# Strassen's seven products for 26 up blocks, planes reloaded in their own place, the first norm by splits

## The chip, the cores and the metric

The kernel runs on one core of a Trainium2 chip. The time is device microseconds from the start to the end of one execution; that of a kernel is the median of several runs. The engines are named as in the profile: PE (matrix unit), PEld (its weight loads), DVE (vector engine), ACT (scalar engine), POOL (a second vector engine), SP (it issues most DMAs). Each engine works through its own queue in order.

## The reference

One inference step of one hybrid decoder layer over 1024 prompt tokens and 8 sample tokens of width 1024: two branches (HGRN2 and Mamba-2) on a normed input, a gated merge, an output projection, and then a feed-forward part (FFN) of inner width 4096, which is where most of the change lies. Everything is float32.

```python
h = _rmsnorm(x, p['norm_mix']) * (1 + sc1) + sh1
proj = h @ p['w_in']
q, f, i, og, z, xbc, dt, ga, gb = jnp.split(proj, IN_OFFSETS, axis=-1)
...
u = jax.nn.sigmoid(ga + bma) * (o_hg @ p['w_br_a']) + jax.nn.sigmoid(gb + bmb) * (y @ p['w_br_b'])
x = x + g1 * (u @ p['w_out'])
h2 = _rmsnorm(x, p['norm_mlp']) * (1 + sc2) + sh2
x = x + g2 * (jnp.square(jax.nn.relu(h2 @ p['w_up'])) @ p['w_down'])
```

## The kernel before

Activations lie transposed: a plane is 128 channels (partitions) by NT = 1032 tokens (1024 prompt and 8 sample), so a width of 1024 is 8 planes. Tokens are cut in NS = 3 splits of SW = 344 columns. A weight block is 128 output channels: a tile of 128 x 1024 that holds 8 blocks of 128 x 128.

Precision is kept by splitting each float32 operand into a high part `hi` (rounded to float32r, on ACT) and a low part `lo` (the rest, on DVE). Each product is then three float32r matmuls, wh·xl, wl·xh and wh·xh. One output block thus takes 3 splits x 8 k-blocks x 3 = 72 matmuls of 344 columns.

`load_w` brings a weight tile into a staging buffer (`stage`, name `wr`, three buffers), and makes `wh` (line 53, ACT) and `wl` (line 55, DVE), two buffers each, at a high priority. `dense_split` (line 86) computes one split, `dense` three. `DenseK` (line 114) instead takes one plane of the input after the other into three or six open accumulators; it is used where the planes only just become ready: at the first norm, and at the two merge products.

The stages in order: modulation (ada) and first norm with the first DenseK (`phase_h`), HGRN2, SSM groups, the merge (`phase_merge`: last gates, `w_br_a`, `w_br_b`), `w_out`, the FFN, a last norm. In the merge, o- and y-planes (`od`, `yd`) and gate planes (`gd`) come back from DRAM; `load_split` loads a plane into a staging buffer and splits it. In the FFN, four chunks follow each other: 8 up blocks, whose results (relu, square) are split and kept in SBUF as `ah`, `al`, then 8 down blocks that read them and add to `x1`.

The program is written with tiles: a scheduler orders each engine's instructions by their priority, and a tile's next writer waits for the readers of the buffer that it reuses. Planes lie in pools by tag ("A", "Q1", "Q2", "Q3").

Of the kernel before, what the change touches and what calls it, by code (L numbers as in the profile page):

```python
# [17 lines left out]
P = 128  # L18
T = 1024
# [18 lines left out]
def cs(s):  # L38
    return slice(s * SW, (s + 1) * SW)


def stage(k):
    return k.wp.tile([P, NT], F32, tag="wr", name="wr", bufs=3)


def load_w(k, src, prio=AHEAD):

    nc = k.nc
    with k.tc.high_priority(prio):
# [3 lines left out]
        nc.scalar.activation(wh, wr, AF.Copy)  # L53
        wl = k.wp.tile([P, KD * P], F32R, tag="wl", name="wl", bufs=2)
        nc.vector.tensor_tensor(wl, wr, wh.bitcast(F32), op=ALU.subtract)  # L55
    return wh, wl
# [21 lines left out]
def dense_split(k, w, X, s, evac, M=P):  # L78
    wh, wl = w
    nc = k.nc  # L80
    acc = k.ps.tile([P, 512], F32, tag="acc", name="acc", bufs=3)
    n = len(X)
    for i, (xh, xl) in enumerate(X):
        sl = slice(i * M, (i + 1) * M)
        for j, (a, b) in enumerate(((wh, xl), (wl, xh), (wh, xh))):
            nc.tensor.matmul(acc[:M, :SW], a[:, sl], b[:, cs(s)],  # L86
                             start=(i == 0 and j == 0), stop=(i == n - 1 and j == 2))
    with k.tc.high_priority(AHEAD):
        evac(s, acc[:M, :SW])


def dense(k, src, X, evac):

    w = load_w(k, src)
    for s in range(NS):
        dense_split(k, w, X, s, evac)


class DenseK:
# [8 lines left out]
    def step(self, xh, xl):  # L108
        k, i = self.k, self.i
        sl = slice(i * P, (i + 1) * P)  # L110
        for (wh, wl), ac in zip(self.ws, self.accs):
            for s in range(NS):
                for j, (a, b) in enumerate(((wh, xl), (wl, xh), (wh, xh))):
                    k.nc.tensor.matmul(ac[s][:, :SW], a[:, sl], b[:, cs(s)],  # L114
                                       start=(i == 0 and j == 0), stop=(i == self.n - 1 and j == 2))
        self.i += 1
        if self.i < self.n:
            return
        with k.tc.high_priority(AHEAD):
            for ev, ac in zip(self.evacs, self.accs):  # L120
                for s in range(NS):
                    ev(s, ac[s][:, :SW])


def split_plane(k, src, tag, hi_name="hi", lo_name="lo"):
    nc = k.nc
    hi = k.pp.tile([P, NT], F32R, tag=tag, name=hi_name)
    nc.scalar.activation(hi, src, AF.Copy)
    lo = k.pp.tile([P, NT], F32R, tag=tag, name=lo_name)
    nc.vector.tensor_tensor(lo, src, hi.bitcast(F32), op=ALU.subtract)  # L130
    return hi, lo
# [146 lines left out]
def phase_h(k, evacs):  # L278


    nc = k.nc
    X = []

    def plane(tag, name):
        return k.pp.tile([P, NT], F32, tag=tag, name=name)
    ss = [rec_ps(k, "ss") for s in range(NS)]
    SUMS = ((0, 1, 2, 3), (4, 5, 6), (7,))
    for kk in range(KD):
        x = plane("B", "x")
# [24 lines left out]
    ws = [ada_load(k, n, (wa(), wa())) for n in range(AH)]  # L314
    for s in range(NS):
        sl = cs(s)
        rstd_from(k, ss[s][:, :SW], SW, 1.0 / 1024, (ra[:, sl], rs[:, sl], rt[:, sl]))
    k.hX = []

    def plane_step(kk):  # L320
        A, sh = scale_shift(k, k.i, kk, k.norm_mix, 0, 8)
        x = X[kk]
        hi = k.pp.tile([P, NT], F32R, tag="A", name="hh")
        lo = k.pp.tile([P, NT], F32R, tag="A", name="hl")

        nc.gpsimd.tensor_tensor(x[:, T:], x[:, T:], A[:, 1:9], op=ALU.mult)
        nc.gpsimd.tensor_tensor(x[:, T:], x[:, T:], rs[:, T:], op=ALU.mult)
        nc.gpsimd.tensor_tensor(x[:, T:], x[:, T:], sh[:, 1:9], op=ALU.add)
        nc.vector.scalar_tensor_tensor(x[:, :T], x[:, :T], A[:, 0:1], rs[:, :T], ALU.mult, ALU.mult)
        nc.scalar.activation(hi[:, :T], x[:, :T], AF.Identity, bias=sh[:, 0:1])  # L330
        nc.scalar.activation(hi[:, T:], x[:, T:], AF.Copy)
        nc.vector.scalar_tensor_tensor(lo[:, :T], x[:, :T], sh[:, 0:1], hi[:, :T].bitcast(F32),
                                       ALU.add, ALU.subtract)
        nc.gpsimd.tensor_tensor(lo[:, T:], x[:, T:], hi[:, T:].bitcast(F32), op=ALU.subtract)
# [495 lines left out]

def load_split(k, src, tag, r=None):
# [29 lines left out]
def phase_merge(k):  # L863
# [8 lines left out]
    oX = []  # L872
    for i in range(KD):
        with k.tc.high_priority(AHEAD):
            oX.append(load_split(k, k.od[i], "A", stage(k)))
        d.step(*oX[i])
    for m in range(2, KD):
        u.append(load_gate(k, m, "Q1"))
# [109 lines left out]
    return x1, h2  # L988


def phase_ffn(k, x1, h2):
    nc = k.nc
    for c in range(4):
        aX, evacs = [], []
        for j in range(KD):
            tag = "A" if j < 4 else "Q3"
            hi = k.pp.tile([P, NT], F32R, tag=tag, name="ah")
            lo = k.pp.tile([P, NT], F32R, tag=tag, name="al")

            def evac(s, ps, hi=hi, lo=lo):  # L1000
                r = k.sp2.tile([P, SW], F32, tag="mt", name="r", bufs=2)
                nc.scalar.activation(r, ps, AF.Relu)  # L1002
                nc.vector.tensor_tensor(r, r, r, op=ALU.mult)  # L1003
                nc.scalar.activation(hi[:, cs(s)], r, AF.Copy)
                nc.vector.tensor_tensor(lo[:, cs(s)], r, hi[:, cs(s)].bitcast(F32), op=ALU.subtract)  # L1005
            evacs.append(evac)
            aX.append((hi, lo))
        up = k.i["w_up"][c * KD:(c + 1) * KD]
        if c == 0:

            ws = [load_w(k, up[j]) for j in range(2)]
            for j, s in [(j, s) for j in range(2) for s in LAST[:2]] + [(0, LAST[2]), (1, LAST[2])]:
                dense_split(k, ws[j], h2, s, evacs[j])
        for j in range(0 if c else 2, KD):
            dense(k, up[j], h2, evacs[j])

        def add(m):
            return lambda s, ps: gated_add(k, s, x1[m][:, cs(s)], x1[m][:, cs(s)], ps, k.modT[:, 40 + m, :])
        if c < 3:
            for m in range(KD):  # L1020
                dense(k, k.i["w_down"][c * KD + m], aX, add(m))
            continue
        for s in LAST:
            acc = k.sp2.tile([P, SW], F32, tag="sqa", name="sqa", bufs=1)
            for m in range(KD):
                w = load_w(k, k.i["w_down"][c * KD + m])
                dense_split(k, w, aX, s, add(m))
                sum_sq(k, acc, x1[m][:, cs(s)], m == 0)
            y = rstd_model(k, acc)
            for m in range(KD):  # L1030
                xx = x1[m][:, cs(s)]
                nc.vector.scalar_tensor_tensor(xx, xx, k.norm_final[:, m:m + 1], y, ALU.mult, ALU.mult)
                nc.sync.dma_start(k.o["y"][m][:, cs(s)], xx)

# [172 lines left out]
```

## Time and profile before

| | us |
|---|---|
| median of three runs | 2561.46 (2558.68 to 2564.11) |
| the profiled execution, its own time | 2561.21 |
| its span | 2559.4 |
| PE busy | 2503.3 (98%) |
| DVE busy | 1642.1 (64%) |
| ACT busy | 1042.8 (41%) |
| first L114 matmul on PE | 35.23 |
| first merge DenseK (`w_br_a` 0 and 1) | 1450.87 to 1473.5 |
| second merge DenseK (`w_br_b` 8 and 9) | 1633.52 to 1656.2 |
| FFN matmuls | about 1820 to 2545 |

Times within an execution are microseconds from the start of its span. The page's chain names what the end waited for, step by step; a row of groups gives line, engine, operation, names, shape, count, busy time and mean ns, and behind the last bar the idle time before it. PE's durations are modelled; its starts are measured, so the interval between two starts is what a matmul costs in a row.

### The profile page before, as it was taken

The numbers are of one execution on the slowest core, as the hardware profiler recorded it, in microseconds if no ns is written. First come the engines' busy times: TensorE is split into PE (matmuls) and PEld (weight loads), VectorE is DVE, ScalarE is ACT, GpSimd is POOL, SyncE is SP. The second block draws the span as 40 slices with busy tenths as digits, with TensorE's granted clock in tenths as the row PEclk, the third lists the DMA queues.
The fourth block names the chain that finished last, engine by engine and source line by source line (L and its number), as shares of the span: only waits on it lengthen the run. The fifth ranks groups of instructions, "written<-read, shape, count | busy, mean of one in ns | idle before, by whom it ended". The sixth has DMA issues, their size and how long they took to land.

```text
span 2559.4 us, 46195 instructions
## 1 busy us (share of the span) xinstructions
PE 2503.3 (98%) x19470; PEld 2439.2 (95%) x19470; DVE 1642.1 (64%) x3314; ACT 1042.8 (41%) x1566; POOL 18.1 (1%) x48
## 2 busy tenths in 40 slices
PE   6999999999999999999999999999999999999998
PEld 5999999889999999999999999999999999999997
DVE  6788888887587687787787744457732332332356
ACT  4455555555444544545545532224520220221333
POOL 2000000000000000000000000000000000000000
PEclk9999999999999999999999999999999999999999
DMA  6322222323333243243343554234211111111134
GB/s 252 102 100 101 101 100 101 101 95 93 93 125 120 90 150 119 99 143 125 101 143 120 195 166 147 75 108 144 88 50 50 42 50 50 42 50 48 43 102 146
DMA packets 92496, 267.04 MB, mean 104 GB/s; under 512 B 16592, under 2 KB 23568, under 8 KB 92272
## 3 DMA queue, kind: packets, MB, share of 16 engines
q1 hardware_dynamic: 91744, 263.08, 31.4%
q8 instruction: 153, 2.51, 0.4%
q0 software_dynamic: 112, 0.66, 0.1%
q14 instruction: 55, 0.45, 0.1%
q10 hardware_dynamic: 432, 0.35, 0.0%
HBM read 224.12 MB, written 40.19 MB: 103 GB/s over the span
## 4 chain that ended last, share of the span: by engine, by line
PE 77%; DVE 2%; ACT 1%; issue 0%; DVEq 0%; ACTq 0%
PE acc L86 68%; PE acc L114 2%; PE y_ps L791 1%; PE yi_ps L795 1%; PE kvx_ps L755 1%; PE xt_ps L743 1%; PE cb_ps L725 1%; DVE wl L55 0%; PE btok_ps L718 0%; PE ss L160 0%; ACT wh L53 0%; PE acc L610 0%; PE ss L161 0%; PE ss L948 0%; DVE sqa L942 0%
## 5 line engine op out<-in xcount | busy, mean ns | idle before, releaser
L86 PE MATMUL acc<-hl,wh 128*128 128x344 f32 x2232 | 720.1, 323 | 0.0
L86 PE MATMUL acc<-hh,wh 128*128 128x344 f32 x2232 | 719.9, 323 | 0.0
L86 PE MATMUL acc<-hh,wl 128*128 128x344 f32 x2232 | 719.3, 322 | 0.0
L86 PEld LDWEIGHTS acc<-hh,wh 128*128 128x128 f32 x2232 | 420.0, 188 | 3.6 <-issue 1.6
L86 PEld LDWEIGHTS acc<-hl,wh 128*128 128x128 f32 x2232 | 419.4, 188 | 3.2
L86 PEld LDWEIGHTS acc<-hh,wl 128*128 128x128 f32 x2232 | 419.3, 188 | 2.8 <-issue 1.4
L53 ACT ACTIVATE wh<-wr 128x1024 fp32r<-128x1024 f32 x224 | 236.5, 1056 | 437.1 <-PE acc L86 360.0
L55 DVE TENSOR_TENSOR wl<-wr,wh 128x1024 fp32r<-128x1024 f32 x224 | 274.1, 1224 | 216.8 <-ACT wh L53 215.9
L86 PE MATMUL acc<-ah,wl 128*128 128x344 f32 x768 | 246.0, 320 | 0.0
L86 PE MATMUL acc<-h2l,wh 128*128 128x344 f32 x768 | 245.9, 320 | 0.0
L86 PE MATMUL acc<-h2h,wl 128*128 128x344 f32 x768 | 245.8, 320 | 0.0
L86 PE MATMUL acc<-al,wh 128*128 128x344 f32 x768 | 245.4, 320 | 0.0
L86 PE MATMUL acc<-h2h,wh 128*128 128x344 f32 x768 | 245.4, 319 | 0.0
L86 PE MATMUL acc<-ah,wh 128*128 128x344 f32 x768 | 245.0, 319 | 0.0
L928 DVE SCALAR_TENSOR_TENSOR x<-acc,modT,x 128x344 f32<-128x344 f32 (+1 forms) x120 | 68.7, 572 | 216.4 <-PE acc L86 216.4
L1003 DVE TENSOR_TENSOR r<-r 128x344 f32<-128x344 f32 x96 | 49.7, 518 | 174.0 <-ACT r L1002 174.0
L86 PE MATMUL acc<-hi,wl 128*128 128x344 f32 x480 | 153.5, 320 | 1.4 <-DVE wl L55 1.4
L86 PE MATMUL acc<-hi,wh 128*128 128x344 f32 x480 | 153.5, 320 | 0.0
L86 PE MATMUL acc<-lo,wh 128*128 128x344 f32 x480 | 152.9, 320 | 0.0
L86 PEld LDWEIGHTS acc<-ah,wh 128*128 128x128 f32 x768 | 144.4, 188 | 0.2
L86 PEld LDWEIGHTS acc<-h2l,wh 128*128 128x128 f32 x768 | 144.5, 188 | 0.0
L86 PEld LDWEIGHTS acc<-al,wh 128*128 128x128 f32 x768 | 144.3, 188 | 0.2 <-DVE al L1005 0.2
(263 smaller groups left out, 4203.2 us busy)
## 6 DMA issues: line engine op xcount, KB each, us to landing
wr<-w_ssm SPq DMA_DIRECT2D x48, 512.0 KB, 3.6
wr<-w_down SPq DMA_DIRECT2D x48, 512.0 KB, 3.6
wr<-w_ada SPq DMA_DIRECT2D x36, 512.0 KB, 3.8
wr<-w_hg SPq DMA_DIRECT2D x32, 512.0 KB, 3.7
w<-cumd SPq DMA_DIRECT2D x32, 512.0 KB, 4.5
wr<-w_up SPq DMA_DIRECT2D x32, 512.0 KB, 3.6
wr<-w_out SPq DMA_DIRECT2D x24, 512.0 KB, 3.6
x<-xT SPq DMA_DIRECT2D x16, 516.0 KB, 4.6
```

The lines of the kernel that those rows point to most:

```text
L53: nc.scalar.activation(wh, wr, AF.Copy)
L55: nc.vector.tensor_tensor(wl, wr, wh.bitcast(F32), op=ALU.subtract)
L86: nc.tensor.matmul(acc[:M, :SW], a[:, sl], b[:, cs(s)], start=(i == 0 and j == 0), stop=(i == n - 1 and j == 2))
L114: k.nc.tensor.matmul(ac[s][:, :SW], a[:, sl], b[:, cs(s)], start=(i == 0 and j == 0), stop=(i == self.n - 1 and j == 2))
L725: nc.tensor.matmul(ps[:, c * P:(c + 1) * P], Bc[:, cc], Cc[:, cc], start=True, stop=True)
L743: nc.tensor.transpose(ps[:, c * P:(c + 1) * P], x[:, cc * P:(cc + 1) * P], k.ident)
L755: nc.tensor.matmul(ps[:, c * P:(c + 1) * P], btok[:, cc], xdec[:, cc], start=True, stop=True)
L791: nc.tensor.matmul(ps[o1:o1 + 64, cc], xdt[:, ci * P + o1:ci * P + o1 + 64], W[:, hh, cc], start=True, stop=True)
L795: nc.tensor.matmul(pi[:, c * P:(c + 1) * P], hs[:, (ci - 1) * P:ci * P], Cc[:, ci * P:(ci + 1) * P], start=True, stop=True)
L928: nc.vector.scalar_tensor_tensor(dst[:, :n], ps[:, :n], gate[:, 0:1], base[:, :n], ALU.mult, ALU.add)
L1003: nc.vector.tensor_tensor(r, r, r, op=ALU.mult)
```

## The change

Four things are changed.

1. FFN up blocks 6 to 31 are computed in 13 pairs by Strassen's scheme (Winograd's form): a pair is a 2 x 2 matrix of weights (2 output blocks, 2 halves of 4 k-blocks) times a 2 x 2 matrix of h2 (2 halves of 4 planes, 2 halves of 516 tokens). Seven products replace eight, each in two quarters of 258 columns. `strassen_weights` makes the weight sums on DVE, `strassen_planes` the sums of h2 (while blocks 2 to 5 run), `strassen_pair` runs products 1, 7, 6, 2, 5, 4, 3. Sums of products are built in the accumulators, and those needed twice are copied out by ACT (`keep`).
2. All 32 up blocks come first; activations are stored to DRAM (`ad`) and loaded again, chunk by chunk, for the down blocks. The first down block is a `DenseK`.
3. `load_split` loads a plane straight into the place of its low part and splits it there, without a staging buffer.
4. The first plane of the first norm is done split by split; the operations on the 8 sample columns move from POOL to DVE; `DenseK.step` loops over splits outside and over weights inside.

```diff
@@ class DenseK, step @@
-        for (wh, wl), ac in zip(self.ws, self.accs):
-            for s in range(NS):
+        for s in range(NS):
+            for (wh, wl), ac in zip(self.ws, self.accs):
@@ phase_h @@
-        nc.gpsimd.tensor_tensor(x[:, T:], x[:, T:], A[:, 1:9], op=ALU.mult)
-        nc.gpsimd.tensor_tensor(x[:, T:], x[:, T:], rs[:, T:], op=ALU.mult)
-        nc.gpsimd.tensor_tensor(x[:, T:], x[:, T:], sh[:, 1:9], op=ALU.add)
-        nc.vector.scalar_tensor_tensor(x[:, :T], x[:, :T], A[:, 0:1], rs[:, :T], ALU.mult, ALU.mult)
-        nc.scalar.activation(hi[:, :T], x[:, :T], AF.Identity, bias=sh[:, 0:1])
...
+        for c in ([slice(s * SW, min((s + 1) * SW, T)) for s in range(NS)] if kk == 0 else [slice(0, T)]):
+            nc.vector.scalar_tensor_tensor(x[:, c], x[:, c], A[:, 0:1], rs[:, c], ALU.mult, ALU.mult)
+            nc.scalar.activation(hi[:, c], x[:, c], AF.Identity, bias=sh[:, 0:1])
+            nc.vector.scalar_tensor_tensor(lo[:, c], x[:, c], sh[:, 0:1], hi[:, c].bitcast(F32),
+                                           ALU.add, ALU.subtract)
...
+        nc.vector.tensor_tensor(xd, xd, A[:, 1:9], op=ALU.mult)
...
@@ load_split @@
-    if r is None:
-        r = stage(k)
-    k.nc.sync.dma_start(r, src)
-    return split_plane(k, r, tag)
+    hi = k.pp.tile([P, NT], F32R, tag=tag, name="hi")
+    lo = k.pp.tile([P, NT], F32R, tag=tag, name="lo")
+    raw = lo.bitcast(F32)
+    nc.sync.dma_start(raw, src)
+    nc.scalar.activation(hi, raw, AF.Copy)
+    nc.vector.tensor_tensor(lo, raw, hi.bitcast(F32), op=ALU.subtract)
+    return hi, lo
@@ new: strassen_weights @@
+        m = [stage(k)[:, :KD * P] for _ in srcs]
+        for t, src in zip(m, srcs):
+            nc.sync.dma_start(t, src)
+        (a11, a12), (a21, a22) = [(t[:, :HK], t[:, HK:]) for t in m]
+        tiles(1, 7)
+        for p in (1, 7):
+            if p == 7:
+                sub(a11, a11, a21)
+            nc.scalar.activation(W[p][0], a11, AF.Copy)
+            sub(W[p][1], a11, W[p][0].bitcast(F32))
+        nc.vector.tensor_tensor(a21, a21, a22, op=ALU.add)
+        sub(a11, a22, a11)
+        wh, wl = tiles(6, 2)
+        nc.scalar.activation(wh, m[0], AF.Copy)
+        sub(wl, m[0], wh.bitcast(F32))
+        wh, wl = tiles(5, 4)
+        nc.scalar.activation(wh, m[1], AF.Copy)
+        sub(wl, m[1], wh.bitcast(F32))
+        sub(a12, a12, a11)
+        tiles(3)
...
@@ new: strassen_pair @@
+    for p, b in ((1, 1), (7, 2), (6, 1), (2, 3), (5, 1), (4, 2), (3, 1)):
+        for q in range(2):
+            acc = bank[b, q]
+            cols = slice(q * HQ, (q + 1) * HQ)
+            wh, wl = W[p]
+            for i, (xh, xl) in enumerate(X[p]):
+                sl = slice(i * P, (i + 1) * P)
+                for j, (a, x) in enumerate(((wh, xl), (wl, xh), (wh, xh))):
+                    nc.tensor.matmul(acc, a[:, sl], x[:, cols], start=(p in (1, 7, 2) and i == 0 and j == 0),
+                                     stop=(i == KD // 2 - 1 and j == 2), skip_group_check=True)
+            with k.tc.high_priority(AHEAD):
+                if p in (1, 6, 7):
+                    keep(p, q, acc)
+                elif p == 2:
+                    evac(0, 0, q, snap[1, q], acc)
...
@@ phase_ffn @@
+    for j in range(2, 6):
+        dense(k, up[j], h2, evac_up(j))
+        strassen_planes(k, h2, T, j - 2)
+    X = strassen_operands(h2, T)
+    for n in range(6, NF, 2):
...
+            else:
+                nc.vector.tensor_tensor(r, a, ps, op=ALU.add)
+                nc.vector.scalar_tensor_tensor(r, r, 0.0, r, ALU.max, ALU.mult)
+            store()
+        strassen_pair(k, (up[n], up[n + 1]), X, evac)
...
+    d = DenseK(k, (down[0],), (add(0),))
+    for j in range(KD):
+        with k.tc.high_priority(AHEAD):
+            aX.append(act(0, j))
+        d.step(*aX[j])
```

How the instructions stand now, at the places where they move. Line numbers of the kernel before are those of the functions above; those of the changed kernel differ (L842 is the load in `load_split`, L1128 the store to `ad`, L1052 the weight load of a pair).

VectorE in the FFN, before: the wl of one up block and three evacuations, over and over.

```order
L1003 TENSOR_TENSOR r<-r 128x344
L55 TENSOR_TENSOR wl<-wr,wh 128x1024
L1005 TENSOR_TENSOR al<-r,ah 128x344
L1003 TENSOR_TENSOR r<-r 128x344
L1005 TENSOR_TENSOR al<-r,ah 128x344
L1003 TENSOR_TENSOR r<-r 128x344
L1005 TENSOR_TENSOR al<-r,ah 128x344
L1003 TENSOR_TENSOR r<-r 128x344
```

After, within the pairs (from the evacuation of product 4 to that of product 2 of the next pair; L1048 and L1060 are weight sums and low parts):

```order
L1157 TENSOR_TENSOR r<-s_21059,b_20974 128x258
L1158 SCALAR_TENSOR_TENSOR r<-r 128x258
L1048 TENSOR_TENSOR wl<-wr,wh 128x512
L1048 TENSOR_TENSOR wr<-wr 128x512
L1132 TENSOR_TENSOR r<-r 128x258
L1060 TENSOR_TENSOR wr<-wr 128x512
L1048 TENSOR_TENSOR wl<-wr,wh 128x512
L1132 TENSOR_TENSOR r<-r 128x258
L1048 TENSOR_TENSOR wr<-wr 128x512
L1048 TENSOR_TENSOR wl<-wr,wh 128x1024
L1048 TENSOR_TENSOR wr<-wr 128x512
L1048 TENSOR_TENSOR wl<-wr,wh 128x1024
```

The low parts of the next pair's weights now stand between the evacuations of this one.

SP at the merge, before: o-planes go into staging buffers (L836), one or two at a time between gate planes (L858).

```order
L836 DMA wr<-od_73 128x1032
L836 DMA wr<-od_74 128x1032
L836 DMA wr<-od_75 128x1032
L858 DMA gt<-gd_96 128x1032
L836 DMA wr<-od_76 128x1032
L858 DMA gt<-gd_97 128x1032
L836 DMA wr<-od_77 128x1032
L836 DMA wr<-od_78 128x1032
L853 DMA gd_111<-gate 128x1032
L836 DMA wr<-od_79 128x1032
L858 DMA gt<-gd_98 128x1032
```

After:

```order
L842 DMA lo<-od_74 128x1032
L866 DMA gt<-gd_98 128x1032
L861 DMA gd_111<-gate 128x1032
L51 DMA wr<-w_br_a 128x1024
L842 DMA lo<-od_75 128x1032
L832 DMA yd_94<-cv 128x1032
L832 DMA yd_95<-cv 128x1032
L842 DMA lo<-od_76 128x1032
L866 DMA gt<-gd_99 128x1032
L842 DMA lo<-yd_81 128x1032
L842 DMA lo<-od_77 128x1032
L842 DMA lo<-yd_84 128x1032
```

Stores that wait for their data (`gd_111`, `yd_94`, `yd_95`) and y-planes now stand ahead of o-planes that the first block still needs.

SP at the way from the up blocks to the first down block, after (`ad_19563` to `ad_19566` are planes 4 to 7 of the first chunk, `ad_19567` and `ad_19568` the next chunk's first two); before, only weights stand here.

```order
L842 DMA lo<-ad_19562 128x1032
L1128 DMA ad_19589<-r 128x258
L51 DMA wr<-w_down 128x1024
L1128 DMA ad_19590<-r 128x258 x2
L842 DMA lo<-ad_19563 128x1032
L1128 DMA ad_19590<-r 128x258 x2
L842 DMA lo<-ad_19567 128x1032
L1128 DMA ad_19589<-r 128x258
L842 DMA lo<-ad_19564 128x1032
L1128 DMA ad_19589<-r 128x258
L51 DMA wr<-w_down 128x1024
L842 DMA lo<-ad_19565 128x1032
```

Loads of planes 5 to 7 stand behind the last pair's stores and a weight.

More of the change, by code (lines that the diff above doesn't have):

```diff
@@ L874, in phase_merge @@
         with k.tc.high_priority(AHEAD):
-            oX.append(load_split(k, k.od[i], "A", stage(k)))
+            oX.append(load_split(k, k.od[i], "A"))
         d.step(*oX[i])
@@ L988, in phase_out, with strassen_planes, sub @@
     return x1, h2
+HN = NT // 2
+HQ = NT // 4
+def strassen_planes(k, h2, T, i):
+    nc = k.nc
+    a, b = stage(k), stage(k)
+    for x, (xh, xl) in ((a, h2[i]), (b, h2[i + 4])):
+        nc.vector.tensor_tensor(x, xh.bitcast(F32), xl.bitcast(F32), op=ALU.add)
+    (b11, b12), (b21, b22) = [(x[:, :HN], x[:, HN:]) for x in (a, b)]
+    def sub(out, x, y):
+        nc.vector.tensor_tensor(out, x, y, op=ALU.subtract)
+    sub(b11, b12, b11)
+    sub(b12, b22, b12)
+    sub(b22, b22, b11)
+    sub(b21, b21, b22)
+    for x, tag, ts in ((a, "A", (1, 3)), (b, "Q3", (4, 2))):
+        p = split_plane(k, x, tag, "th", "tl")
+        for n, t in enumerate(ts):
+            T[t].append(tuple(y[:, n * HN:(n + 1) * HN] for y in p))
@@ L991, in phase_ffn @@
 def phase_ffn(k, x1, h2):
     nc = k.nc
-    for c in range(4):
[L994 to L1018, printed above, removed]
-        if c < 3:
[L1020 to L1033, printed above, removed]
@@ new lines, in phase_ffn, with out, relu2 @@
+    NF = 4 * KD
+    up = k.i["w_up"]
+    ad = [k.dp.tile([P, NT], F32, name="ad%d" % j) for j in range(NF)]
+    bufs = iter(range(1 << 20))
+    def out(j, cols):
+        n = next(bufs) % 4
+        pool, tag = (k.sp2, "mt") if n < 2 else (k.sp, "sq")
+        r = pool.tile([P, SW], F32, tag=tag, name="r", bufs=2)[:, :cols.stop - cols.start]
+        return r, lambda: nc.sync.dma_start(ad[j][:, cols], r)
+    def relu2(r, ps):
+        nc.scalar.activation(r, ps, AF.Relu)
+        nc.vector.tensor_tensor(r, r, r, op=ALU.mult)
@@ new lines, in evac_up, with f @@
+    def evac_up(j):
+        def f(s, ps):
+            r, store = out(j, cs(s))
+            relu2(r, ps)
+            store()
+        return f
+    ws = [load_w(k, up[j]) for j in range(2)]
+    for j, s in [(j, s) for j in range(2) for s in LAST[:2]] + [(0, LAST[2]), (1, LAST[2])]:
+        dense_split(k, ws[j], h2, s, evac_up(j))
+    T = {n: [] for n in (1, 2, 3, 4)}
+    for j in range(2, 6):
+        dense(k, up[j], h2, evac_up(j))
+        strassen_planes(k, h2, T, j - 2)
+    X = strassen_operands(h2, T)
@@ new lines, in phase_ffn, with evac, add @@
+    for n in range(6, NF, 2):
+        def evac(m, half, q, a, ps, n=n):
+            c = half * HN + q * HQ
+            r, store = out(n + m, slice(c, c + HQ))
+            if a is None:
+                relu2(r, ps)
+            else:
+                nc.vector.tensor_tensor(r, a, ps, op=ALU.add)
+                nc.vector.scalar_tensor_tensor(r, r, 0.0, r, ALU.max, ALU.mult)
+            store()
+        strassen_pair(k, (up[n], up[n + 1]), X, evac)
+    def add(m):
+        return lambda s, ps: gated_add(k, s, x1[m][:, cs(s)], x1[m][:, cs(s)], ps, k.modT[:, 40 + m, :])
@@ new lines, in act @@
+    def act(c, j):
+        tag = "A" if c % 2 == 0 else "Q2" if j < 4 else "Q3"
+        return load_split(k, ad[c * KD + j], tag)
+    down = k.i["w_down"]
+    aX = []
+    d = DenseK(k, (down[0],), (add(0),))
+    for j in range(KD):
+        with k.tc.high_priority(AHEAD):
+            aX.append(act(0, j))
+        d.step(*aX[j])
+    for c in range(4):
+        nX = []
+        for m in range(KD):
+            if c == 3:
+                break
+            if c or m:
+                dense(k, down[c * KD + m], aX, add(m))
+            nX.append(act(c + 1, m))
+        if c < 3:
+            aX = nX
@@ new lines, in phase_ffn @@
+    for s in LAST:
+        acc = k.sp2.tile([P, SW], F32, tag="sqa", name="sqa", bufs=1)
+        for m in range(KD):
+            w = load_w(k, down[3 * KD + m])
+            dense_split(k, w, aX, s, add(m))
+            sum_sq(k, acc, x1[m][:, cs(s)], m == 0)
+        y = rstd_model(k, acc)
+        for m in range(KD):
+            xx = x1[m][:, cs(s)]
+            nc.vector.scalar_tensor_tensor(xx, xx, k.norm_final[:, m:m + 1], y, ALU.mult, ALU.mult)
+            nc.sync.dma_start(k.o["y"][m][:, cs(s)], xx)
```

50 lines of the change are left out of this document (45 added, 5 removed).

## The prediction

> **What bounds the kernel now.** I read the page first: PE is busy for 98% of the span, and the chain that ends last runs through one line, L86, the matmul of `dense_split`.
>
> ```profile
> span 2559.4 us, 46195 instructions
> ...
> PE 2503.3 (98%) x19470; PEld 2439.2 (95%) x19470; DVE 1642.1 (64%) x3314; ACT 1042.8 (41%) x1566; POOL 18.1 (1%) x48
> ...
> PE 77%; DVE 2%; ACT 1%; issue 0%; DVEq 0%; ACTq 0%
> ```
>
> An average over stages says little, so the chain in order of time comes next, at the places that the change touches (start, length, what).
>
> ```profile
> 1448.36 23.12 PE acc L114 x146
> 1471.50 1.92 DVE gt L869 x4
> 1473.81 1.23 DVE wl L55
> 1475.09 158.59 PE acc L86 x1005
> 1633.68 20.94 PE acc L114 x132
> 1656.44 1.15 DVE wl L55
> ...
> 1821.84 664.85 PE acc L86 x4224
> 2487.43 30.19 PE acc L86 x192
> ```
>
> From 1821.84 on PE runs 4224 matmuls without one break: 664.85/4224 = 157.4 ns each. Time there is only the number of matmuls by the interval between them; nothing that VectorE, ScalarE or the DMAs do is on the path. The merge stage (1448 to 1473, 1633 to 1657) is matmul-bound too, but each of its two `DenseK` blocks ends in a short wait for VectorE (wl L55).
>
> **The up blocks, the large term.** A pair costs 2 blocks of 8 x 3 splits x 3 = 144 matmuls of 344 columns now: 22.66 us. After, it is 7 products x 2 halves x 4 k-blocks x 3 = 168 matmuls of 258 columns. So everything hangs on the interval at 258 columns, which no row shows. These rows of PE (start, modelled duration, what) and windows bound it; the last four figures of a window are its clock, DMA share and GB/s.
>
> ```profile
> 36.25 0.49 PE L114 MATMUL acc<-hl,wh 128*128 128x344 f32 x1
> 38.55 0.46 PE L114 MATMUL acc<-hh,wh 128*128 128x344 f32 x1
> 38.83 0.33 PE L114 MATMUL acc<-hl,wh 128*128 128x344 f32 x1
> 39.94 0.32 PE L114 MATMUL acc<-hh,wl 128*128 128x344 f32 x1
> 1329.68 1.16 PE L795 MATMUL yi_ps<-cv,hs 128*128 128x128 f32 x8
> 1330.60 0.40 PE L86 MATMUL acc<-hh,wl 128*128 128x344 f32 x1
> ```
> ```profile
> 36.25:38.55 2.30, 2.30 (x10) 2.30 (x10) 2.12 (x6) 0.00 (x0) 0.38 (x2) 0.50 0.56 223
> 1821.00:2487.00 666.00, 666.00 (x4229) 665.30 (x4229) 240.64 (x431) 160.54 (x275) 0.00 (x0) 1.00 0.17 51
> ```
>
> From 36.25 to 38.55 lie 8 intervals at a clock of 0.50: 287.5 ns each; the 7 from 38.83 to 39.94, at the full clock, are 158.6, and the long run above gives 157.4, not half of 287.5, which is 143.75. So some 13.6 ns at the full clock are not cycles of the array, and they vanish when the array is slow. Three readings follow.
> - A supply that gives at most 344/157.4 = 2.19 columns per ns. Then 258 columns take 118.1 ns, a pair 19.83 us: 2.83 saved, over 13 pairs 36.8.
> - Those 13.6 ns are fixed: 258/344 x 143.75 + 13.6 = 121.4 ns, a pair 20.40: 29.4 in all.
> - A floor by the weight load: eight matmuls of 128 columns take 0.92 us at L795, 115 ns each. That would be the best case, 19.32 per pair: 43.5.
>
> I take the first: a fixed extra would show at half clock too, which it does not. 29 and 44 stay the ends. The break-even interval is 22.66/168 = 134.9 ns.
>
> The Trainium skill (TensorE: Matmul & The Clock Gate, section Back-to-back issue gap) has a rule that speaks against the change: in a stream of weight loads and matmuls it gives 81 ns at 128 columns and 131 at 512, so a matmul of 258 columns saves little over one of 344. By that slope, 0.13 ns per column, the estimate here is 157.4 - 11.2 = 146.2 ns and a pair 24.56 us, 24.7 us lost over 13 pairs. The trace disagrees with its level (157.4 ns at 344, where the rule gives 109), which is why I give its shape a small chance only.
>
> **What has to keep up inside a pair.** Durations of VectorE and ScalarE in the same stretch (mean ns in the second last column):
>
> ```profile
> L55 DVE TENSOR_TENSOR wl<-wr,wh 128x1024 fp32r<-128x1024 f32 x64 | 78.4, 1226 | 22.1 <-ACT wh L53 22.1
> L53 ACT ACTIVATE wh<-wr 128x1024 fp32r<-128x1024 f32 x64 | 67.7, 1058 | 262.4 <-PE acc L86 246.0 <-issue 16.4
> L1003 DVE TENSOR_TENSOR r<-r 128x344 f32<-128x344 f32 x96 | 49.7, 518 | 174.0 <-ACT r L1002 174.0
> L1002 ACT ACTIVATE r<-acc 128x344 f32<-128x344 f32 x96 | 44.0, 459 | 200.5 <-PE acc L86 200.5
> ```
> ```profile
> wr<-w_up SPq DMA_DIRECT2D x32, 512.0 KB, 3.6
> ```
>
> VectorE per pair: seven operations of 512 columns at half of 1.226 = 4.3, two of 1024 = 2.5, fourteen evacuation steps of 258 at 518 x 258/344 = 389 ns = 5.4: 12.2 us of 19.8. ScalarE: 512+512+1024+1024+512 columns at 1.058 per 1024 = 3.7, and eight evacuations of 344 ns = 2.8: 6.5. Neither is the bound, but queues run in order, so the tightest hand-over counts. A product takes 24 x 118 = 2.83 us. The weights of the next pair's product 1 reuse the buffer that product 4 frees, one product (2.83 us) ahead. Behind its end on VectorE stand the evacuations of product 4's second half (2 x 0.39), then wl (0.61): ready 1.6 us after, 1.2 us spare. Product 7 has 1.7 us spare, products 6 and 2 1.2, 5 and 4 3.3. Two weight loads and eight stores make 2.1 MB per pair, 106 GB/s; the stores sit behind loads on SP, but the four-buffer ring leaves room. I cost this at nothing. If the cover is gone the bound is one spare missed: a loss of 1 us in each pair would take 13 of the 37.
>
> The planes for Strassen (blocks 2 to 5): per plane pair 4 operations of 1024 and 4 of 516, 7.4 us, four times 30 us of VectorE, beside 4 x 11.3 = 45 us of matmuls in which those blocks' own work is 4 x (1.23 + 1.55) = 11 us. Covered; 0 to 1 us.
>
> **First merge block, reload in place.** Before, the o-planes go ahead through three staging buffers. Now each can start its load only when a plane of the first norm has had its last use, step by step in the gate block that ends at 1450.7, and conversion follows the load in the same plane.
>
> ```profile
> 1450.70:1473.70 23.00, 23.00 (x148) 22.82 (x147) 14.74 (x20) 18.38 (x20) 0.00 (x0) 1.00 0.93 312
> ```
> ```profile
> 1460.05 1.23 DVE L130 TENSOR_TENSOR lo<-wr,hi 128x1032 fp32r<-128x1032 f32 x1 [1.53 <-ACT hi L128]
> 1462.81 1.23 DVE L130 TENSOR_TENSOR lo<-wr,hi 128x1032 fp32r<-128x1032 f32 x1 [0.44 <-ACT hi L128]
> 1466.14 1.23 DVE L130 TENSOR_TENSOR lo<-wr,hi 128x1032 fp32r<-128x1032 f32 x1
> ```
> ```profile
> wr<-od SPq DMA_DIRECT2D x5, 516.0 KB, 4.0
> gt<-gd SPq DMA_DIRECT2D x4, 516.0 KB, 6.9
> ```
>
> DMA is already busy for 0.93 here at 312 GB/s, and the last o-plane's low part comes at 1466.14+1.23 = 1467.4, where its step starts at 1450.9 + 7 x 2.83 = 1470.7: 3.3 us spare. In the new order the o-loads share SP with gate planes, waiting stores and y-planes between them; at 1.3 to 1.7 us a plane (528 KB at 400 or 312 GB/s) and 4 to 6.9 us to land I get the last low part at about 1477, and the block ends 6 us late (0 to 8). Behind it, the next weight's wl stands on VectorE after six gated evacuations instead of the four in the chain above: +1.8 (0 to 2). The second block's y-planes are freed late in the same way, but only in its last steps: +1.5 (0 to 2).
>
> **Way out of the FFN up part.** Activations now go to DRAM and come back. The first down chunk's planes 4 to 7 can only be loaded once product 5 of the last pair has ended, two products (5.7 us) before the end, with stores, a weight and the next chunk's planes between them on SP. Four loads and their companions, about 8 x 1.3 = 10.4 us plus 4.0 to land and 2.3 to convert, against 5.7 + 4 steps of 2.83: steps 5 to 7 wait about 5 us in all (1 to 8). Later chunks have 90 us of lead. 34 MB more DRAM traffic beside 51 GB/s is nothing.
>
> **Start.** The rows show 3.7 us of VectorE over three whole planes, ScalarE held by POOL, then PE.
>
> ```profile
> 28.68 3.68 DVE L329 SCALAR_TENSOR_TENSOR x<-x,modA,rs 128x1024 f32<-128x1024 f32 x3
> 32.61 0.21 ACT L331 ACTIVATE hh<-x 128x8 fp32r<-128x8 f32 x1 [8.40 <-POOL x L328]
> 35.23 0.65 PE L114 MATMUL acc<-hl,wh 128*128 128x344 f32 x1 [4.80 <-DVE hl L332]
> 61.35 1.14 ACT L330 ACTIVATE hh<-x,modT 128x1024 fp32r<-128x1024 f32 x1
> 62.52 1.28 DVE L332 SCALAR_TENSOR_TENSOR hl<-x,modT,hh 128x1024 fp32r<-128x1024 f32 x1 [1.66 <-ACT hh L330]
> 63.86 0.42 PE L114 MATMUL acc<-hl,wh 128*128 128x344 f32 x1 [1.84 <-DVE hl L332]
> ```
>
> Now a third of the first plane is enough, so PE starts near 30. But the last step still waits for the last plane on VectorE (1.84 us at 63.86), which only comes earlier by what the modulation chain on PE and the POOL hop give: I take 2.6 us (0.5 to 4.8), less 0.9 because the new loop order of `DenseK` releases a weight 3 matmuls before the end instead of 9. Net -1.7.
>
> **Sum.** 2561.2 (the profiled execution's own time; 0.3 from the median, 2561.46) - 36.8 - 1.7 + 6 + 1.8 + 1.5 + 5 = 2537.0. A change of 0.2%, 5 us, is about what a measurement can tell here.
>
> **Rivals.**
> - *The interval falls less than the columns* (slower). One mechanism: each matmul carries a cost that does not shrink. The straight line from 115 ns at 128 columns to 157.4 at 344 gives 140.5 ns at 258, a pair 23.60 us: +12.3, and with the 12.6 of the other terms 2586. At a width-free 157.4 it is 26.44 per pair, 2623. With the 12.6 it decides at 129.1 ns. For it: no 258-column row exists. Against: the half-clock rows, where matmuls scale as N. Chance 0.09. The page's rule above belongs here.
> - *Fixed extra of 13.6 ns*: 2544. Chance 0.2.
> - *Reloads hidden* (SP's queue runs further ahead than I think, or planes come at 400 GB/s): without the 6 and the 5 it is 2526; with the weight-load floor also 2519. Chance 0.15.
> - *Waits inside a pair*, VectorE in order: 1 us per pair 2550, from 1.9 us per pair no gain (2562). For it: three spares of 1.2 to 1.7 us rest on sums of durations without queue delays. Against: VectorE idles 7 us per pair. Chance 0.08.
>
> My forecast has 0.48, its own range 2529 to 2546. Leaving out the first rival and the far ends of the others, the range is 2519 to 2556. Faster: 0.48 + 0.2 + 0.15 + 0.04; same 0.03; slower 0.10.
>
> **What would show it.** Right: in the FFN a gap-free row of PE with some 2200 matmuls of 258 columns about 118 ns apart; the wait of 4.80 at the first L114 gone, PE starting near 30; PE waits for the low parts of o-planes after 1455 and of reloaded planes at the first down block. Wrong: intervals above 129 ns, a wait of PE for wl inside pairs that comes back thirteen times, or merge waits far above 8 us.

## The result, and the profile after

| | before | after |
|---|---|---|
| median of the runs, us | 2560.49 (4 runs) | 2544.32 (2541.63 to 2546.80, 4 runs) |
| the profiled execution, us | 2561.21 | 2545.65 |
| its span, us | 2559.4 | 2543.9 |

The ratio is 0.9935 (95% interval 0.9922 to 0.9947): 16 us faster, where 24 had been forecast. The profiled executions differ by 15.5 us in their spans, and the terms below are made against that.

The page of the changed kernel: engines, and the chain by engine and line.

```profile
PE 2476.2 (97%) x19782; PEld 2408.9 (95%) x19782; DVE 1755.5 (69%) x3513; ACT 1065.1 (42%) x1574; POOL 4.2 (0%) x16
...
PE 74%; DVE 3%; DMA 2%; ACT 1%; issue 1%; SPq 0%; DVEq 0%; ACTq 0%
```

PE has 312 more instructions and 27 us less to do. New in the chain is DMA with 2%. The chain in order of time shows where it stands (start, length, what):

```profile
1436.72 5.40 DMA lo<-od
1454.91 7.84 DMA gt<-gd
1462.82 10.18 DMA lo<-od
1481.40 156.37 PE acc L86 x983
1643.36 18.74 PE acc L114 x117
1666.73 101.14 PE acc L86 x640
1802.00 28.23 PE acc L86 x179
1830.92 65.40 PE acc L86 x413
1896.33 258.65 PE b L1102 x2157
2154.97 4.93 DMA lo<-ad
2165.62 9.77 DMA lo<-ad
2178.28 293.72 PE acc L86 x1867
```

The one row of before from 1821.84 has become four pieces: plain up blocks, the pairs, the first down block, and the other down blocks. The thirteen pairs are a single stretch of PE (line 1102) with no break; the way into the merge (1436 to 1478) and the way out of the up blocks (2155 to 2178) now hang on DMAs of planes. The waits of PE in those two stretches (us in total, times, longest; inside the pairs there are none), and the busy times of PE, PEld, DVE, ACT and POOL there, with the clock, the DMA share and GB/s at the end (first the merge, then the pairs, then the way out):

```profile
PE acc L114 <- DVE lo L844: 6.3, 6, 2.4
PE acc L86 <- ACT wh L53: 0.7, 1, 0.7
...
PE acc L114 <- DVE lo L844: 4.9, 3, 2.1
PE acc L114 <- DVE wl L55: 1.4, 1, 1.4
```
```profile
1436.00:1478.00 42.00, 35.67 (x216) 33.54 (x215) 27.70 (x37) 30.11 (x39) 0.00 (x0) 1.00 0.93 352
1896.33:2158.10 261.77, 261.77 (x2185) 261.77 (x2184) 164.33 (x296) 92.57 (x172) 0.00 (x0) 1.00 0.37 114
2158.00:2178.00 20.00, 13.71 (x75) 12.36 (x73) 12.45 (x14) 10.12 (x11) 0.00 (x0) 0.91 0.94 346
```

In the pairs PE is busy for all of 261.77 us: PE waited for no weight, no evacuation and no store there, although VectorE worked 164 of them. In the other two stretches the DMAs are at 0.93 and 0.94 of their time.

Where the 15.5 us come from, by the same landmarks in both traces (first and last matmul of each piece):

| term | forecast | in the trace |
|---|---|---|
| 13 pairs | -36.8 | -32.7 |
| start, as far as the dt stage keeps it | -1.7 | -3.3 (-5.5 at the end of the first DenseK) |
| first merge block and its next weight | +7.8 | +11.0 |
| second merge block and its next weight | +1.5 | +1.5 |
| way out of the up blocks | +5 | +8.9 |
| blocks 0 to 5, with the planes for Strassen | 0 | +0.6 |
| tail and the rest | 0 | -1.5 |
| sum | -24.2 | -15.5 |

### The profile page after: what moved, and what is told of

Read it like the earlier page. It is cut to its first block, busy times and chain, and to the rows that moved or that the text cites. A ratio compares the mean times of both kernels' runs of the same rounds, so it can differ in the third digit from the quotient of the medians.

```text
span 2543.9 us, 47439 instructions
## 1 busy us (share of the span) xinstructions
PE 2476.2 (97%) x19782; PEld 2408.9 (95%) x19782; DVE 1755.5 (69%) x3513; ACT 1065.1 (42%) x1574; POOL 4.2 (0%) x16
## 4 chain that ended last, share of the span: by engine, by line
PE 74%; DVE 3%; DMA 2%; ACT 1%; issue 1%; SPq 0%; DVEq 0%; ACTq 0%
PE acc L86 56%; PE b L1102 10%; PE y_ps L794 1%; PE yi_ps L798 1%; PE kvx_ps L758 1%; PE acc L114 1%; DMA lo<-od 1%; PE xt_ps L746 1%; DMA lo<-ad 1%; PE cb_ps L728 1%; DVE wl L55 0%; DMA gt<-gd 0%; ACT wh L53 0%; PE btok_ps L721 0%; PE acc L613 0%
## 5 line engine op out<-in xcount | busy, mean ns | idle before, releaser
L86 PE MATMUL acc<-hi,wl 128*128 128x344 f32 x1224 | 392.5, 321 | 2.3 <-DVE wl L55 2.3
L86 PE MATMUL acc<-lo,wh 128*128 128x344 f32 x1224 | 391.1, 320 | 1.5 <-ACT wh L53 1.4
L86 PE MATMUL acc<-hi,wh 128*128 128x344 f32 x1224 | 391.5, 320 | 0.0
L86 PEld LDWEIGHTS acc<-hi,wl 128*128 128x128 f32 x1224 | 230.3, 188 | 3.1 <-DVE wl L55 2.9
L86 PEld LDWEIGHTS acc<-lo,wh 128*128 128x128 f32 x1224 | 230.3, 188 | 2.4 <-ACT wh L53 2.0
L86 PEld LDWEIGHTS acc<-hi,wh 128*128 128x128 f32 x1224 | 230.6, 188 | 0.2
L678 DVE SCALAR_TENSOR_TENSOR cv<-raw,cst,cv 128x1024 f32<-128x1024 f32 x96 | 122.8, 1279 | 0.0
L1102 PE MATMUL b<-tl,wh 128*128 128x258 f32 x416 | 117.7, 283 | 0.0
L1102 PE MATMUL b<-th,wl 128*128 128x258 f32 x416 | 117.4, 282 | 0.0
L1102 PE MATMUL b<-th,wh 128*128 128x258 f32 x416 | 117.4, 282 | 0.0
L670 ACT ACTIVATE raw<-acc 128x344 f32<-128x344 f32 x96 | 42.9, 456 | 126.0 <-PE acc L86 125.4
## 6 DMA issues: line engine op xcount, KB each, us to landing
ad<-r SPq DMA_DIRECT2D x104, 129.0 KB, 1.9
```

Source lines behind the costliest of these rows:

```text
L86: nc.tensor.matmul(acc[:M, :SW], a[:, sl], b[:, cs(s)], start=(i == 0 and j == 0), stop=(i == n - 1 and j == 2))
L670: dense(k, w, k.hX, lambda s, ps: nc.scalar.activation(raw[:, 3 + s * SW:3 + (s + 1) * SW], ps, AF.Copy))
L678: nc.vector.scalar_tensor_tensor(cv[:, :T], raw[:, j:j + T], cw[:, j:j + 1], cv[:, :T], ALU.mult, ALU.add)
L1102: nc.tensor.matmul(acc, a[:, sl], x[:, cols], start=(p in (1, 7, 2) and i == 0 and j == 0), stop=(i == KD // 2 - 1 and j == 2), skip_group ...
```

## The experiments

Each kernel was timed beside the kernel before on its own chip, so ratios are compared: 0.9935 for the changed kernel, and 0.9934 (0.9922 to 0.9947) when it was run once more, unaltered, as a control:

> The changed kernel once more, unaltered, beside the next two on one chip. Nothing is changed, so 2544 (2541 to 2547), and of its trace: the first merge block from the start of the last gate block to its end about 43 us, the first down block 20 us against 11.3 of matmuls.

It came out at 2543.31 us, with 42.3 us for the stretch up to the end of the first merge block and 19.0 for the first down block, both as they are measured below.

**What a matmul of 258 columns costs.**

```diff
+    rb = k.pp.tile([P, NT], F32R, tag="A", name="rb")
+    nc.scalar.activation(rb, x1[KD - 1], AF.Copy)
...
+    for n, (width, count) in enumerate([(344, 96)] + [(v, 48) for v in (128, 160, 192, 216, 240, 258, 280, 300, 344, 400, 430, 512)]):
...
+        for i in range(count):
+            nc.tensor.matmul(acc[:, :width], (wh, wl)[i % 2][:, i % 8 * P:(i % 8 + 1) * P], rb[:, :width],
+                             start=(i == 0), stop=(i == count - 1))
...
```

> After the end of the changed kernel, PE runs series of 48 float32r matmuls of one width each (128 to 512 columns, another weight each time, nothing else busy), ahead of them 96 of 344 columns to warm the clock. The total time means nothing. In the changed kernel 344 columns take 157.3 ns from start to start and 258 take 119.9. Supply theory (2.19 columns per ns): 240 columns 110, 280 128, 300 137, 400 183, 512 234 ns. Fixed theory (13.6 ns and 0.418 ns per column): 280 131, 300 139, 400 181, 512 228. Line through the two measured points (7.7 ns and 0.435 ns per column): 280 129.5, 300 138.2, 400 181.7, 512 230.4. If 258 columns here take clearly less than 119.9, the pairs wait for something else than the array. Below some width a floor of 112 to 115 ns by the weight load should show, at 128 and 160 columns above all.

Rows of PE in that tail: the first matmul of the widths 240, 258 and 280 and of 344 and 400 columns. A series has 48, so the distance between two such rows is 48 intervals.

```profile
2577.78 0.28 PE L1202 MATMUL n<-rb,wh 128*128 128x240 f32 x1
2583.16 0.28 PE L1202 MATMUL n<-rb,wh 128*128 128x258 f32 x1
2589.02 0.29 PE L1202 MATMUL n<-rb,wh 128*128 128x280 f32 x1
...
2601.87 0.32 PE L1202 MATMUL n<-rb,wh 128*128 128x344 f32 x1
2609.40 0.34 PE L1202 MATMUL n<-rb,wh 128*128 128x400 f32 x1
```

5.38 us for 240 columns is 112.1 ns each, 5.86 for 258 is 122.1, 7.53 for 344 is 156.9. All series, as the mean of 47 intervals in ns:

```
columns   128    160    192    216    240    258    280    300    344    400    430    512
ns      110.5  111.9  111.9  111.9  112.0  122.1  129.0  138.7  157.0  183.4  196.7  233.2
```

Up to 240 columns the width does not matter: the floor is 112 ns. From 280 on it is 2.16 to 2.20 columns per ns, the supply that the half-clock rows had pointed to; the fixed 13.6 ns would have given 228 at 512 columns, against 233.2 measured, and 131 at 280, against 129.0. At 258, just above the floor, 122.1 is 4 more than the proportion gives. The pairs ran at 119.9, no slower than this series with nothing else busy, so VectorE, ScalarE and the DMAs do not hold them up. The slope estimated from the two figures of the Trainium skill (TensorE: Matmul & The Clock Gate, section Back-to-back issue gap: 81 ns at 128 columns, 131 at 512), 0.13 ns per column, is not seen with these float32r matmuls: between 344 and 512 columns it is 0.454.

**What Strassen's pairs are worth.**

```diff
-        strassen_pair(k, (up[n], up[n + 1]), X, evac)
+        for j in (n, n + 1):
+            dense(k, up[j], h2, evac_up(j))
```

> The changed kernel with its 26 up blocks as plain blocks of 72 matmuls of 344 columns (the sums for Strassen's planes are still made, and not used). Theory (the pairs gain by their matmuls alone, 168 x 119.9 against 144 x 157.4 ns): 32.7 us more, 2577 (2574 to 2580). Rival (the pairs also cost time at their ends, by VectorE or SP): then less than 32 are lost, and the waits at the first down block shrink too, 2568 to 2573.

2573.33 us, ratio 1.0049 (1.0034 to 1.0065): 29 more than the changed kernel. This lies between the two, just above the rival's range. In the traces the 26 blocks take 33 us more of matmuls, and the first down block is 3 us shorter (17.3 against 20.2; 19.0 in the control). So the pairs gain by their matmuls, and a small part of that may be lost again right behind them. Without Strassen the rest of the change would have made the kernel slower by half a per cent (the sums of h2's planes are still made in this run).

**The first merge block.** Between the first matmul of the gate block ahead of it and its own last matmul lie 34.9 us before and 42.9 after. Three kernels vary what could make the difference. All planes through the staging buffers again:

```diff
-        oX.append(load_split(k, k.od[i], "A"))
+        oX.append(load_split_staged(k, k.od[i], "A", stage(k)))    # likewise for the y-planes
```

> Only the o- and y-planes of the merge go through the staging buffers again, as before the change; the FFN keeps its reload in place. Theory (the place that a load has to wait for makes the merge late): the two merge DenseK blocks and their next weights get back 11.0 and 1.5 us, so 2532 (2530 to 2536). Rival (the merge is late because of what the changed FFN or the earlier start brings to SP and the DMAs): no change, 2544.

2535.29 us, ratio 0.9907 (0.9893 to 0.9921), and the stretch is 34.9 again. The rival fell; the sum was 3 us short, and the waits for weights behind the two blocks are mostly still there: 2.7 us against 3.7 (below). Then only the y-planes:

> As the changed kernel, but the y-planes of the merge go through the staging buffers again; the o-planes, which the first merge block waits for, still load in the place of their low part. Theory A (y-planes that load without a staging buffer are issued early and share the DMAs with the o-planes): nearly all of the 8 us in the first merge block come back, 2536 to 2538. Theory B (an o-plane has to wait for the place that the gate block frees): the block stays 6 to 8 us late, 2542 to 2545.

2543.41 us, ratio 0.9933 (0.9920 to 0.9945): nothing gained in the medians, as theory B has it. Its profiled execution, the fastest of its five, has 38.8 in the stretch and 3.0 us of waits for o-planes instead of 6.3, which fits neither theory. And only the o-planes:

> The counterpart of the run with the y-planes staged: the o-planes go through the staging buffers, the y-planes load in place. Theory A (the y-planes' early loads take the DMAs' time): the first merge block stays about 4 us late, 2539 to 2541. Theory B (an o-plane waits for the place that the gate block frees): no lateness is left, 2534 to 2537, as with all planes staged.

2535.51 us, ratio 0.9901 (0.9885 to 0.9916), as good as with all planes staged. The stretch is 36.6 in its profiled execution, the slowest of its four; PE's waits there show no o-plane any more, but a gate:

```profile
PE acc L114 <- ACT gate L861: 1.7, 1, 1.7
PE acc L86 <- ACT wh L53: 0.7, 1, 0.7
PE acc L86 <- DVE wl L55: 0.5, 1, 0.5
```

So it is the o-planes' own place that decides. How it does so is shown only in part. SP's waits in the changed kernel, from 1430 to 1480:

```profile
SPq L861 <- ACT gate L854: 13.0, 2, 8.3
SPq L842 <- PE acc L114: 0.7, 2, 0.4
```

Directly, SP waits only 0.7 us for PE to release a plane's place (L842). It waits 13.0 us for gates whose store (L861) stands ahead of loads; 8.3 of them stand there before the change too, and the other 4.7 come just ahead of the fourth o-plane. Most of the lateness thus lies in where the scheduler put the loads in SP's queue. That the place is the reason for this position is argued from the last run, which changes only where the o-planes load. ScalarE's rows in the changed kernel show the planes as they arrive (each conversion waits for its DMA, named in brackets):

```profile
1461.49 1.07 ACT L843 ACTIVATE hi<-lo 128x1032 fp32r<-128x1032 f32 x1 [2.84 <-DMA lo<-od]
1462.78 1.06 ACT L867 ACTIVATE gt<-gt 128x1032 f32<-128x1032 f32 x1 [0.22 <-DMA gt<-gd]
1464.08 1.07 ACT L843 ACTIVATE hi<-lo 128x1032 fp32r<-128x1032 f32 x1 [0.23 <-DMA lo<-yd]
1465.36 1.07 ACT L843 ACTIVATE hi<-lo 128x1032 fp32r<-128x1032 f32 x1 [0.21 <-DMA lo<-od]
1466.63 1.06 ACT L843 ACTIVATE hi<-lo 128x1032 fp32r<-128x1032 f32 x1 [0.21 <-DMA lo<-yd]
1467.91 1.07 ACT L867 ACTIVATE gt<-gt 128x1032 f32<-128x1032 f32 x1 [0.22 <-DMA gt<-gd]
1469.18 1.07 ACT L843 ACTIVATE hi<-lo 128x1032 fp32r<-128x1032 f32 x1 [0.20 <-DMA lo<-od]
...
1473.02 1.07 ACT L843 ACTIVATE hi<-lo 128x1032 fp32r<-128x1032 f32 x1 [0.15 <-DMA lo<-od]
```

A plane arrives every 1.28 us, in the order of issue, and only every third is one that the running block needs: between two o-planes come two others, of gates or y. At 1.28 us a step of 2.83 us could be fed twice over; at three times that it cannot, and PE's last steps there start 3.8 to 3.9 us apart. The transfers' times say the same (KB each, median us to landing; 4.0 for o-planes and 6.9 for gate planes before):

```profile
lo<-od SPq DMA_DIRECT2D x8, 516.0 KB, 6.0
gt<-gd SPq DMA_DIRECT2D x8, 516.0 KB, 10.2
lo<-yd SPq DMA_DIRECT2D x6, 516.0 KB, 9.7
```

How much of the 8 us the y-planes alone carry is not settled: the one trace without their early loads says about half, the medians say nothing.

**The order of the loops in DenseK.**

```diff
-        for s in range(NS):
-            for (wh, wl), ac in zip(self.ws, self.accs):
+        for (wh, wl), ac in zip(self.ws, self.accs):
+            for s in range(NS):
```

> As the changed kernel, with the loop order of DenseK as before the change (weights outside, splits inside). Theory: the new order releases the first weight of two later, and each of the two merge blocks ends with PE waiting for the next wh (0.67 and 0.72 us in the trace); these waits go, and the second block's 1.5 us with them, 2541.5 to 2543.5. Rival (the second block is late by its y-planes, as the prediction said): the waits stay. At the start, the old order needs all splits of a plane sooner: up to 1 us back.

2538.78 us, ratio 0.9921 (0.9907 to 0.9934), nearly 3 us below the theory's lower end. PE's waits behind the second merge block, first of the changed kernel, then of this one:

```profile
PE acc L86 <- DVE wl L55: 0.8, 1, 0.8
PE acc L86 <- ACT wh L53: 0.7, 1, 0.7
```
```profile
PE acc L86 <- DVE wl L55: 0.6, 1, 0.6
```

The wait for wh is gone here and behind the first block, where wl also falls from 1.5 to 0.8: together 2.3 us, of the 3.3 by which the ratio lies below the control's (0.0013 of 2560; the intervals overlap, so the rest may be nothing). The first DenseK ends at 61.0 as in the changed kernel: the new order brought nothing there.

**The way out of the up blocks.** Two weight blocks for the first down DenseK:

```diff
-    d = DenseK(k, (down[0],), (add(0),))
+    d = DenseK(k, (down[0], down[1]), (add(0), add(1)))
...
-            if c or m:
+            if c or m > 1:
```

> The first down DenseK takes two weight blocks at once (down 0 and 1), so a plane has 5.66 us of matmuls ahead of it instead of 2.83; the same matmuls in all. Theory (planes 4 to 7 come late one behind the other, at 3.5 to 5 us each): the 8.9 us lost there shrink to 1 to 3, so 2537 to 2539. Rival (the planes' loads start late as a whole, behind the stores of the last pair): the first late plane makes the same wait, and 4 or more stay, 2540 to 2544.

2536.23 us, ratio 0.9905 (0.9892 to 0.9919): the theory's 2537 to 2539, slightly passed. The block takes 25.3 us (144 matmuls are 22.7), 2.6 of waits where the changed kernel has 8.9, and nothing waits for a plane's low part:

```profile
PE acc L114 <- DVE wl L55: 0.8, 1, 0.8
PE acc L86 <- ACT wh L53: 0.7, 1, 0.7
PE acc L86 <- DVE wl L55: 0.7, 1, 0.7
PE acc L114 <- ACT wh L53: 0.4, 1, 0.4
```

A step of this block is 18 matmuls, 2.83 us, with two weight blocks and 9 matmuls, 1.42 us, with one (not 5.66 and 2.83, as the expectation has it). With two, plane 7 is needed only 19.8 us after the block's start; in the control it was in use 17.2 us after it. So the run shows that two weight blocks cover the planes' lateness; it can't tell loads that come one behind the other from loads that start late as a whole, since both would be covered.

Is it the next chunk's planes that hold planes 4 to 7 up? They were sent through the staging buffers:

```diff
-        return load_split(k, ad[c * KD + j], tag)
+        return (load_split_staged if c == 1 else load_split)(k, ad[c * KD + j], tag)
```

> As the changed kernel, but the second chunk's eight planes, which are not needed for 90 us, load through the staging buffers and so cannot all be sent off beside the first chunk's. Theory A (those loads share the DMAs with planes 4 to 7): the first down block comes down from 20 us to 15 to 17, 2539 to 2541. Theory B (planes 4 to 7 start late, behind the last pair's stores): it stays at 19 to 20, 2543 to 2545.

2545.44 us, ratio 0.9939 (0.9926 to 0.9951), beside the control's 0.9934; the block takes 17.9 us against the control's 19.0 (20.2 in the first trace), with 4.3 us of waits for three planes against 5.7. The company thus costs 1 to 2 us in the traces and nothing that the medians show. Most of the lateness stays without it, which fits the late start behind the last pair's stores; no run moves those stores, so this cause is argued.

**The start alone.** The kernel before with the new first norm (lines 326 to 334 of before replaced by those of the diff), the old loop order and nothing else:

> The kernel before with the new first norm alone (first plane by splits, the eight sample columns on VectorE), the old order of DenseK and nothing else. Theory: PE starts at about 30 instead of 35.2 and the first DenseK ends 5 us earlier; 3 to 5 us of it reach the end, 2555.5 to 2557.5. Rival (the HGRN heads that follow give it back, since they wait for VectorE and DMAs anyway): 2559 to 2561.

2553.25 us (11 runs), ratio 0.9977 (0.9969 to 0.9986): 5.7 us, more than the theory's upper end.

**All that helped in one kernel.** The merge's planes staged, two weight blocks in the first down DenseK, the new loop order only at the start:

> The changed kernel with all of the merge's planes staged, two weight blocks in the first down DenseK, and the new loop order of DenseK only at the start. If the parts add up (9.0 by the staging, 8 by the two weights, 1 to 2 by the order): 2526 to 2529. If they share a cause (a better state of that chip, or the same DMA queue): 2531 to 2535.

2527.27 us, ratio 0.9875 (0.9862 to 0.9889): the parts add up, as far as such intervals can tell. From the first merge block to the first down block PE's only waits of note are for wl, 2.9 us in three places and 1.3 in one:

```profile
PE acc L86 <- DVE wl L55: 2.9, 3, 1.5
PE acc L119 <- DVE wl L55: 1.3, 1, 1.3
```

This kernel is faster than the one before and than the changed one, than the latter by some 15 us (0.0060 of 2560).

## Why the prediction was right or wrong

- **The pairs.** Right in mechanism, and the rivals on the slow side are out: 2184 matmuls, no break, 119.9 ns. The size was off by 1.8 ns per matmul, 4 us in all: 258 columns lie just above the 112 ns floor, and the proportion 2.19 holds, within about 1%, only from 280 columns on. The floor that I took from L795 (115 ns) was nearly right, but I used it only as a best case and did not ask what happens close to it.
- **Neighbours inside a pair.** "I cost this at nothing" held, with smaller spares than worked out: VectorE took 164 of 262 us (0.63, where 12.2 of 19.8 had been worked out), with its operations of 512 and 258 columns at about 690 and 425 ns instead of the 613 and 389 scaled by width:

```profile
L1158 DVE SCALAR_TENSOR_TENSOR r<-r 128x258 f32<-128x258 f32 x78 | 33.4, 428 | 2.6
L1048 DVE TENSOR_TENSOR wl<-wr,wh 128x512 fp32r<-128x512 f32 x39 | 26.7, 685 | 0.0
```

- **First merge block.** The step "the block ends 6 us late (0 to 8)" named the right wait, with 8.0 measured. Its order of arrival was right too; what I mis-sized is how many planes not yet needed arrive between two o-planes. What follows it, put at +1.8 for the next weight, cost 3.0 in this trace and 1.5 in the control's; with the old loop order it is nothing. The 1.5 between the two traces is the clock's, which the sum had not: right behind the waits for wh and wl (0.67 and 1.48 us) it was granted at 0.50, and the matmuls lay 286 ns apart instead of 157. The control, with the same waits, has no such stretch there.

```profile
1482.15:1485.30 3.15, 3.15 (x12) 3.15 (x12) 1.48 (x2) 0.80 (x1) 0.00 (x0) 0.50 0.80 251
```

  I had charged the loop order at the start (0.9), where the run with the old order shows nothing of it, and not here.
- **Second merge block.** The number was right (+1.5) and the cause wrong: "y-planes are freed late" does not show in the trace; no plane is waited for. The loop order releases the weights late, and with the old order 0.6 us of waits is left, as much as before the change.
- **Way out of the up blocks.** The wait was the right one (planes 4 to 7, whose loads stand behind the last pair's stores on SP), the term too small: 8.9 instead of 5, and 7.2 to 9.4 in the other traces where nothing of it was altered. As written, the sum gives no wait at all: 10.4 + 4.0 + 2.3 = 16.7 us of loading against 5.7 + 4 x 2.83 = 17.0. A step with one weight block is 9 matmuls, 1.42 us, so the cover is 11.4, and only that leaves about 5. PE's waits for planes were 4.9 in this trace and 5.7 in the control's, so the 5 is a good size that does not follow from its own sum. The wait for wl at the first step (0.6 to 1.7 where there was one) was missing, and the last plane took 9.8 us to land, not 4.0.
- **Start.** Too small: I let PE begin 5 us earlier and then let the last plane, on VectorE, take half of it back. Before, each plane waits for POOL, and planes come every 4.96 us while PE needs 4.06 for a step with its modulation products. After, they come every 4.48, and PE, which starts earlier, waits no more than 0.07 us for one in this trace (once 0.61 in the control's). VectorE's rows, of before and of after (the low part of the last two planes):

```profile
57.56 1.28 DVE L332 SCALAR_TENSOR_TENSOR hl<-x,modT,hh 128x1024 fp32r<-128x1024 f32 x1 [1.66 <-ACT hh L330]
62.52 1.28 DVE L332 SCALAR_TENSOR_TENSOR hl<-x,modT,hh 128x1024 fp32r<-128x1024 f32 x1 [1.66 <-ACT hh L330]
```
```profile
52.50 1.28 DVE L329 SCALAR_TENSOR_TENSOR hl<-x,modT,hh 128x1024 fp32r<-128x1024 f32 x1 [0.73 <-ACT hh L328]
56.99 1.29 DVE L329 SCALAR_TENSOR_TENSOR hl<-x,modT,hh 128x1024 fp32r<-128x1024 f32 x1 [0.74 <-ACT hh L328]
```

  I had counted the hop over POOL once, as the lower end of 0.5 us, and it is in every plane: ScalarE idled 3.71 us for POOL ahead of the last one. In the profiled execution 2.2 us of the 5.5 went again in the first HGRN heads; how much is kept differs: at the gate block ahead of the first merge block the other traces with the same start lie between 0.4 and 6.2 us ahead of the kernel before. One sign did not come true: PE does start near 30, but the wait at its first L114 matmul is not gone, it is 3.73 us where it was 4.80.

```profile
29.68 0.66 PE L114 MATMUL acc<-hl,wh 128*128 128x344 f32 x1 [3.73 <-DVE hl L329]
```

The forecast of 2537 was 7 us too low, within its own range (2529 to 2546): the pairs, the merge and the way out were each 3 to 4 us worse, the start 1.6 better. The rival with a fixed extra of 13.6 ns had 2544, which is what came out, but by chance: it needs pairs that gain 29.4 us, they gained 32.7, and the widths refute it (233.2 ns at 512 columns where it gives 228). The mechanism of the large term was right; that the total stayed in the range owes something to errors of about 1.5 us each at the start and in the tail that went the other way.

## What to carry to other kernels

Fewer columns per matmul pay in proportion only well above the width at which the interval stops falling (240 columns here); measure the interval at the new width before counting matmuls. Taking a staging buffer away saves bytes but is not free: the load is then bound to the release of its place, and it can end up in the queue behind loads that go earlier and are needed later. Where a block starts before its planes are there, giving each plane two weight blocks to feed doubles the time that the next plane may take, at no cost in matmuls.

## What the runs showed of the hardware

- Float32r matmuls with a new weight each have a floor of 112 ns from start to start up to 240 columns, and run at 2.16 to 2.20 columns per ns from 280 to 512 columns at the full clock. What sets the floor is not shown. Why the supply stops at 2.19, below the 2.4 that twice the half-clock rate would be (344 columns in 287.5 ns at a clock of 0.50), is not shown.
- Between 240 and 258 columns the interval jumps by 10 ns for 18 columns, to 122.1; inside the kernel the same shape ran at 119.9. Why these two differ is open.
- With the DMAs full (a share of 0.93 around the first merge block), planes of 516 KB arrived in order of issue, one every 1.28 us, whoever waited for them.
- Two short waits of PE (0.67 and 1.48 us) were followed, in one trace, by 3.15 us at a granted clock of 0.50, which cost 1.5 us; the control's trace has the same waits and full clock behind them. What decides it is not shown.
